# Three edits at the end of attention, and two splits of q in other steps

## The chip, the cores and the metric

The kernel runs on one core of one Trainium2 chip. Five engines work side by side, each through its own list of instructions in order: PE (TensorE) multiplies matrices and turns tiles, DVE (VectorE) and ACT (ScalarE) do elementwise work, POOL (GpSimd) does a little of it and issues some transfers, SP (SyncE) issues most transfers. They meet at semaphores. The metric is the device time of one execution, in microseconds (us): a median over runs. Beside it stands one profiled execution, whose trace gives every instruction's start and length; all rows below are from that trace, in us from the start of its span.

## What is computed

One block of a streaming encoder over 1024 tokens of width 1024, all in float32; branch a is the gated convolution `ya`, branch b causal attention `yb` with 8 heads of 64:

```python
def mixer(h, w_in, b_f, conv_w, w_branch, w_out):
    ...
    proj = jnp.einsum("bsd,dn->bsn", h, w_in)
    q, k, v, f_logit, g_b, g_c, hc, gate_conv, gate_attn = jnp.split(proj, _SPLITS, axis=-1)
    ya = g_b * causal_depthwise_conv(g_c * hc, conv_w)
    ...
    logf = jax.nn.log_sigmoid(f_logit.astype(jnp.float32) + b_f.astype(jnp.float32))
    yb = forgetting_attention(q.reshape(shp), k.reshape(shp), v.reshape(shp), logf)
    yb = yb.reshape(bsz, s_len, ATTN_WIDTH)
    ya_d = jnp.einsum("bsc,cd->bsd", ya, w_branch[0])
    yb_d = jnp.einsum("bsc,cd->bsd", yb, w_branch[1])
    merged = jax.nn.sigmoid(gate_conv) * ya_d + jax.nn.sigmoid(gate_attn) * yb_d
    return jnp.einsum("bsd,de->bse", merged, w_out)
...
        h = rmsnorm(x, norm_mix_pre[l])
        m = mixer(h, w_in[l], b_f[l], conv_w[l], w_branch[l], w_out[l])
        x = x + rmsnorm(m, norm_mix_post[l])
        h = rmsnorm(x, norm_ffn_pre[l])
        f = swiglu(h, w_gate_up[l], w_down[l])
        x = x + rmsnorm(f, norm_ffn_post[l])
```

## The kernel before

Every float32 product is made of three products of split operands: a tensor is cut into a high part (copied on ACT) and a low part (the rest, subtracted on DVE), and PE adds high by high, high by low and low by high into one bank (`mm3`, line 125). The stages are: norm and v; the input projections (which store q, k, `ya` and the gates to DRAM); attention, with branch a's products filled in between; branch b; the output projection with its norms; the gated feed-forward.

**The attention loop** (line 1236) has 24 units of work, `NU`, and runs over steps t from 2 to 25. A unit is a pair of heads j and one or two blocks of 128 rows (`steps`, line 880): heads 0 to 2 have six units each, from row block 7 down to the pair (1, 0), and the last pair has the units 18 to 23. The loop is a pipeline. In step t PE makes the scores of unit t (`sp`), turns the rows of unit t - 1 (`tps`, the weights after the exponential, in 128x128 tiles, up to four to a bank) and multiplies the turned rows of unit t - 2 by v (`pv_pair`, into `po`). DVE adds the bias and takes row maxima (`pt,nm<-sp,cb`), ACT takes the exponentials, and both copy turned rows out of their banks (`ptT<-tps`; `turn_bank` issues the turns and returns the copy as a function; `da` to `dd` are the four of one step, first head then second). In this stage `strict` holds all five engines to the order in which the program is written.

**What fills the steps.** Branch a is cut into groups (d, n): 128 output columns d by 512 tokens n, each in four quarters of three products (`branch_a`, line 1099, tile `pba`). The table `units` gives how many quarters a step takes. The quarters go into one bank, `mb`, one group after the other; the last quarter of a group returns a function, the multiply of the bank by a gate into `um`, and this frees the bank. A step's quarters are issued ahead of `dc` and `dd`. What is left of the step, in this order, is the copies `dc` and `dd`, the exponentials, then three lists:

```python
        for f in lows + muls + at.pop(t, []):
            f()
```

`lows` are the subtractions of the splits whose copies were made earlier in the step (table `cuts`: splits of q, k, `ya` and weights), `muls` are the multiplies, and `at` holds loads and a few others (tables at lines 1200 to 1234). Loads of `raw` tiles share three buffers.

**The inverse rows.** When a pair of heads has all its row sums, DVE takes their reciprocals (`ri`), PE turns them (`tr<-ident,ri`), DVE copies them (`rT`), SP stores them (`ri_dram`) and loads them back spread over the partitions (`rb`), and DVE multiplies `yb` by them (`divide`). For the last pair the reciprocal is in step 24 and the turn in step 25, `NU + 1`.

**Banks.** PSUM has eight here. The pool `pst` (line 671) has two, `ma` (holds `po`) and `mb`; `pss` (line 994) has six, four for scores (`S`) and two for turned tiles (`T`). After the loop both pools close, and `psm2` (line 1291) hands out all eight in turn. Its first three tiles are the three groups of branch a that are left, (7, 0), (6, 1) and (7, 1), between the splits of `yb` and the last divides; then come the groups of branch b (`pbb`).

Of the kernel before, what the change touches and what calls it, by code (L numbers as in the profile page):

```python
# [10 lines left out]
F32 = mybir.dt.float32  # L11
# [6 lines left out]
P = 128  # L18
# [4 lines left out]
NC = 512  # L23
# [22 lines left out]
def block_kernel(  # L46
# [16 lines left out]
    n1, n2 = slice(0, NC), slice(NC, S)  # L63
# [29 lines left out]
    def pool(name, bufs=1, side="left", space=None):  # L93
        kw = dict(name=name, bufs=bufs)
        if space is not DRAM:
            kw["reuse_waits"] = "tile"
        if space is not None:
            kw["space"] = space
        else:
            kw["side"] = side  # L100
        stack = ExitStack()
        ctx.callback(stack.close)
        return stack.enter_context(tc.tile_pool(**kw)), stack.close
# [10 lines left out]
    def mul(o, a, b):  # L114
        nc.vector.tensor_tensor(o, a, b, op=ALU.mult)
# [4 lines left out]
    def split(hi, lo, src):  # L120

        copy(hi, src)
        sub(lo, src, f32(hi))

    def mm3(ps, a, b, start, stop, **kw):

        ah, al = a
        bh, bl = b
        nc.tensor.matmul(ps, ah, bh, start=start, stop=False, **kw)
        nc.tensor.matmul(ps, ah, bl, start=False, stop=False, **kw)  # L130
        nc.tensor.matmul(ps, al, bh, start=False, stop=stop, **kw)

    cpool, _ = pool("const")
    stat, _ = pool("stat", 4, side="right")
    dpool, _ = pool("dram", space=DRAM)
# [355 lines left out]
    wpool, _ = pool("w")  # L491
# [134 lines left out]
    def strassen(w, hb, psp, tmp, p1=None):  # L626

        b1 = None
        if p1 is None:
            b1 = bank(psp, "b1")  # L630
            prod(b1, w["A11"], hb[B11], True)
            p1 = t_(tmp, "c21")
            copy(p1, b1)
        b2, b3 = bank(psp, "b2"), bank(psp, "b3")
        prod(b2, w["S2"], hb[T2], True)
        c12 = t_(tmp, "c12")
        add(c12, p1, b2)
        prod(b3, w["S1"], hb[T1], True)
        c22 = t_(tmp, "c22")
        add(c22, p1, b3)  # L640
        if b1 is not None:
            prod(b1, w["A12"], hb[B21], False)
        prod(b2, w["S3"], hb[T3], False)
        add(c22, c22, b2)
        prod(b3, w["S4"], hb[B22], False)
        add(c12, c12, b3)
        prod(b2, w["A22"], hb[T4], False)
        c21 = p1
        add(c21, p1, b2)
        return b1, c12, c21, c22  # L650
# [21 lines left out]
    psm, psm_close = pool("psm", 6, space=PSUM)  # L672
# [121 lines left out]
    def groups(t):  # L794

        rows_ = steps[t][1]
        if len(rows_) == 1:
            return [[(rows_[0], 0)], [(rows_[0], 1)]]
        return [[(i, 0), (i, 1)] for i in rows_]
# [4 lines left out]
    def mask_of(t, i):  # L804

        j = steps[t][0]
        for e in range(2):
            c = row_of(j, i, e)[:, i * P : (i + 1) * P]
            nc.gpsimd.tensor_tensor(c, c, mask, op=ALU.add)
# [72 lines left out]
    NU = len(steps)  # L882
    sps, nms, ps_, ptTs = {}, {}, {}, {}

    def step_qk(t):
        j, rows_ = steps[t]
        if j not in rsums:
            rsums[j] = t0_.tile([P, 2 * ST], F32, tag="rsum", name="rsum", bufs=2)
        for i in rows_:
            sps[t, i] = qk(j, i)  # L890
# [56 lines left out]
    for ij, (kind, j, _, _) in enumerate(jobs):  # L947
# [4 lines left out]
        if ij < 2:  # L952
# [29 lines left out]
            _, c12, c21, c22 = strassen(w, h1b, psm, pp, p1)  # L982
# [7 lines left out]
        else:  # L990
# [3 lines left out]
            pss, pss_close = pool("pss", space=PSUM)  # L994
# [104 lines left out]
    def branch_a(d, n, psp, tag):  # L1099

        ns = (n1, n2)[n]
        ps = psp.tile([P, NC], F32, tag=tag, name="pba")
        wh, wl = was[d]
        for k in range(4):
            mm3(
                ps, (wh[:, k, :], wl[:, k, :]), (ya2[n][0][:, k, :], ya2[n][1][:, k, :]),
                k == 0, k == 3,
            )
            yield None if k < 3 else lambda: mul(um[:, d, ns], sgs[d, n], ps)
# [16 lines left out]
    def inverse_rows(j, psp, tag, bufs=1):  # L1126

        tr = psp.tile([P, 4, P], F32, tag=tag, name="tr", bufs=bufs)[: 2 * ST, 0, :]
        nc.tensor.transpose(tr, invs[j], ident)

        def drain():
            rT = t1.tile([2 * ST, P], F32, tag="rT", name="rT", bufs=2)
            nc.vector.tensor_copy(rT, tr)
            for e in range(2):
                nc.sync.dma_start(
                    ri_dram[j][e].rearrange("(i p) -> i p", p=P), rT[e * ST : (e + 1) * ST, :]
                )
            rb = rbs[j] = tp_.tile([P, S], F32, tag="rb", name="rb", bufs=1)
            for e in range(2):
                nc.sync.dma_start(  # L1140
                    rb[e * HD : (e + 1) * HD, :], ri_dram[j][e].partition_broadcast(HD)
                )

        return drain
# [3 lines left out]
    def pv_pair(t):  # L1148
        j, rows_ = steps[t]
        k0 = 0  # L1150
        for i in rows_:
            if i % 4 == 3:
                po[0] = pst.tile([P, 4, P], F32, tag="ma", name="po")
            for k in range(i + 1):
                for e in range(2):
                    nc.tensor.matmul(
                        po[0][e * HD : (e + 1) * HD, i % 4, :],
                        vs_[j][:, k, e * HD : (e + 1) * HD],
                        ptTs[t, e][:, k0 + k, :],
                        start=(k == 0),  # L1160
                        stop=(k == i),
                    )
            k0 += i + 1
            if i % 4 == 0:
                copy(
                    yb[:, j, i * P : (i + 4) * P].rearrange("p (a b) -> p a b", a=4),
                    po[0],
                )
# [27 lines left out]
    def do(f, *args):  # L1196
        return lambda: f(*args)
# [1 line left out]

    cuts, at = defaultdict(list), defaultdict(list)  # L1200
    for j, parts in (
        (1, ((2, "k", n1), (3, "k", n2), (4, "q", n2), (5, "q", n1))),
        (2, ((9, "k", n1), (10, "k", n2), (11, "q", n2), (13, "q", n1))),
        (3, ((14, "k", n1), (15, "q", n1), (16, "k", n2), (17, "q", n2))),
    ):
        cuts[parts[0][0]].append(do(qk_tiles, j))
        for t, what, c in parts:
            cuts[t].append(do(split_q if what == "q" else split_k, j, c))
# [8 lines left out]
    at[2].append(do(q_load, 1))  # L1217
    for t, j in ((7, 2), (13, 3)):
        at[t] += [do(load_kv, j), do(q_load, j)]
    for t, n, m in ((2, 0, 0), (3, 0, 2), (3, 1, 0), (6, 1, 2)):  # L1220
        at[t].append(do(load_ya, n, m))
    for d, t in enumerate((2, 6, 8, 11, 13, 17, 20, 23)):
        at[t].append(do(load_wa, d))
# [12 lines left out]
    for t in range(2, NU + 2):  # L1236
        turned = None
        now = groups(t) if t < NU else ([], [])
        back = t - 1 if t <= NU else None
        wide = back and sum(i + 1 for i in steps[back][1]) > 6  # L1240
        if t < NU:
            step_qk(t)
        if 6 < t <= NU:
            pv_pair(t - 2)
        if t in rows:
            turned = inverse_rows(rows[t], pst, "mb")
        if t == NU + 1:
            inverse_rows(3, pss, "T", 2)()
        if back:
            da = turn_bank(back, 0, 0, "ACT")  # L1250
            db = turn_bank(back, 0, 1, "DVE")
            da()
        if t <= 6:
            pv_pair(t - 2)
        for i, e in now[0]:
            row_max(t, i, e)
        if t < NU and len(steps[t][1]) > 1:
            mask_of(t, steps[t][1][1])
        if turned:
            turned()  # L1260
        if back and db:
            db()
        if t == NU:
            inverse(3)
        for i, e in now[0]:
            expo(t, i, e)
        lows = [f for f in (g() for g in cuts.pop(t, ())) if f]
        muls = [m for m in (next(fill, None) for _ in range(units.get(t, 0))) if m]
        if back:
            dc = turn_bank(back, 1, 0, "ACT" if wide else "DVE")  # L1270
            dd = turn_bank(back, 1, 1, "DVE" if wide else "ACT")
        for i, e in now[1]:
            row_max(t, i, e)
        if back:
            dc()
            if dd:
                dd()
        for i, e in now[1]:
            expo(t, i, e)
        if t > NU:  # L1280
            pv_pair(t - 2)
        if t + 1 < NU:
            mask_of(t + 1, steps[t + 1][1][0])
        for f in lows + muls + at.pop(t, []):
            f()
# [5 lines left out]
    psm, psm_close = pool("psm2", 8, space=PSUM)  # L1291
    t1_close()

    def yb_split(n, ks):
        ns = (n1, n2)[n]
        for k in ks:
            split(yb2[n][0][:, k, :], yb2[n][1][:, k, :], yb[:, k, ns])

    for m in branch_a(KT - 1, 0, psm, "mm"):
        pass  # L1300
    for n in range(2):
# [187 lines left out]
    for f in range(NF):  # L1489
        if f < NPRE:  # L1490
# [4 lines left out]
            _, g2, u1_, u2 = strassen(rest.get(), hb, psm, fp, p1)  # L1495
# [270 lines left out]
```

## Time and profile before

| | us |
|---|---|
| median of 3 runs | 1341.31 (1341.25 to 1341.66) |
| the profiled execution's own time | 1342.25 |
| its span | 1340.5 |
| PE busy | 1322.3 (99%) |
| DVE busy | 935.7 (70%) |
| ACT busy | 540.2 (40%) |
| POOL busy | 127.8 (10%) |

A row of a timeline gives the start, the length, the engine, the line, the operation, out<-in, the shape and a count; a bracket at its end gives how long the engine had been idle just before and what ended that. All rows have line 75, which is the helper through which every instruction is recorded, so names tell the place. Products of PE overlap: one starts about 0.23 us after another but is shown as 0.39 long. A row of SP is the issue of a transfer, not the transfer.

### The profile page before, as it was taken

How to read it: one execution, taken by the hardware profiler on the slowest of the kernel's cores; microseconds unless marked ns; L12 is line 12 of the kernel's file. 1: busy time of each engine (PE TensorE's matmuls, PEld its weight loads, DVE VectorE, ACT ScalarE, POOL GpSimd, SP SyncE). 2: the span in 40 equal slices, each digit the busy share in tenths (PEclk: the TensorE clock that was granted, in tenths of full speed). 3: DMA queues.
4: the chain of work that ended last, by engine and by line, in shares of the span. 5: the costliest groups of instructions: out<-in, count | busy, mean ns of one | idle time of the engine just before them, and what ended most of it. 6: DMA issues, size and time to landing. Idle time of an engine off the chain costs nothing. (4 is left out here: it accounts for less than half of the span.)

```text
span 1340.5 us, 17724 instructions
## 1 busy us (share of the span) xinstructions
PE 1322.3 (99%) x6737; PEld 1096.9 (82%) x6737; DVE 935.7 (70%) x1464; ACT 540.2 (40%) x879; POOL 127.8 (10%) x252
## 2 busy tenths in 40 slices
PE   8999999999999999999999999999999999999997
PEld 7988888888887888788887788888888888888886
DVE  6983767755446767675669898677677766677585
ACT  8641322143346756514446322223222323444452
POOL 0011000011112212000002121110011001000000
PEclk9999999999999999999999999999999999999999
DMA  6342422343325445362235554332333336966541
GB/s 206 99 130 87 138 60 82 116 121 99 108 89 173 158 142 190 110 213 79 95 121 186 180 195 143 104 116 75 105 111 110 102 103 248 366 231 197 158 166 63
DMA packets 153558, 186.88 MB, mean 139 GB/s; under 512 B 9448, under 2 KB 106800, under 8 KB 153472
## 3 DMA queue, kind: packets, MB, share of 16 engines
q1 hardware_dynamic: 138736, 137.20, 32.9%
q0 software_dynamic: 14736, 48.54, 9.4%
q8 instruction: 53, 0.87, 0.3%
q14 instruction: 33, 0.27, 0.1%
HBM read 136.62 MB, written 49.09 MB: 139 GB/s over the span
## 5 line engine op out<-in xcount | busy, mean ns | idle before, releaser
L75 DVE TENSOR_TENSOR c<-c,b 128x512 f32<-128x512 f32 x195 | 133.2, 683 | 87.3 <-PE b L75 68.4
L75 DVE TENSOR_TENSOR lo<-raw,hi 128x1024 fp32r<-128x1024 f32 (+1 forms) x93 | 112.1, 1206 | 80.9 <-PE b L75 69.0
L75 ACT ACTIVATE hi<-raw 128x1024 fp32r<-128x1024 f32 (+1 forms) x100 | 101.9, 1019 | 124.6 <-PE b L75 77.2
L75 ACT ACTIVATE hi<-sx 128x1024 fp32r<-128x1024 f32 x41 | 43.6, 1063 | 237.3 <-PE b L75 209.2
L75 PE MATMUL b<-hth,hi 128*128 128x512 f32 x352 | 137.1, 389 | 0.3 <-DVE c L75 0.3
L75 PE MATMUL b<-hth,lo 128*128 128x512 f32 x352 | 137.1, 389 | 0.2 <-DVE lo L75 0.2
L75 PE MATMUL b<-htl,hi 128*128 128x512 f32 x352 | 137.0, 389 | 0.0
L75 PEld LDWEIGHTS b<-hth,hi 128*128 128x128 f32 x352 | 66.1, 188 | 14.5 <-DVE c L75 0.7
L75 PEld LDWEIGHTS b<-hth,lo 128*128 128x128 f32 x352 | 66.1, 188 | 14.2 <-DVE lo L75 0.6
L75 PEld LDWEIGHTS b<-htl,hi 128*128 128x128 f32 x352 | 66.1, 188 | 13.7
L75 DVE TENSOR_TENSOR lo<-sx,hi 128x1024 fp32r<-128x1024 f32 x41 | 50.2, 1224 | 30.8 <-PE b L75 29.4
L75 PE MATMUL b<-hah,hi 128*128 128x512 f32 x176 | 68.7, 393 | 1.5 <-ACT c L75 1.5
L75 PE MATMUL b<-hal,hi 128*128 128x512 f32 x176 | 68.5, 389 | 0.0
L75 PE MATMUL b<-hah,lo 128*128 128x512 f32 x176 | 68.4, 389 | 0.0
L75 DVE TENSOR_TENSOR sx<-raw 128x512 f32<-128x512 f32 x78 | 53.7, 689 | 19.1 <-DMA raw<-in_w_in_dram 8.8
L75 PE MATMUL pd<-hi,lo 128*128 128x512 f32 x160 | 62.3, 389 | 0.0
L75 PE MATMUL pd<-hi 128*128 128x512 f32 x160 | 61.9, 390 | 0.0
L75 PE MATMUL pd<-ghi 128*128 128x512 f32 x148 | 57.6, 390 | 0.0
L75 PE MATMUL pd<-glo,ghi 128*128 128x512 f32 x148 | 57.6, 389 | 0.0
L75 PE MATMUL pd<-ghi,glo 128*128 128x512 f32 x148 | 57.6, 389 | 0.0
L75 PE MATMUL b<-hT34h,hi 128*128 128x512 f32 x136 | 53.0, 390 | 0.4 <-DVE c L75 0.4
L75 PE MATMUL b<-hT34h,lo 128*128 128x512 f32 x136 | 52.9, 389 | 0.0
(380 smaller groups left out, 3366.6 us busy)
## 6 DMA issues: line engine op xcount, KB each, us to landing
raw<-in_w_gate_up_dram SPq DMA_DIRECT2D x51, 512.0 KB, 3.8
raw<-in_w_in_dram SPq DMA_DIRECT2D x35, 512.0 KB, 3.8
a_dramS<-um POOLq DMA_DIRECT2D x44, 256.0 KB, 2.7
a_dramA<-um POOLq DMA_DIRECT2D x33, 256.0 KB, 2.8
sg<-sg_dram SPq DMA_DIRECT2D x32, 256.0 KB, 4.5
xt<-in_x_dram SPq DMA_DIRECT2D x15, 512.0 KB, 4.6
graw<-a_dramS SPq DMA_DIRECT2D x14, 512.0 KB, 3.9
sg_dram<-c POOLq DMA_DIRECT2D x24, 256.0 KB, 2.3
```

What stands on the lines that cost most here:

```text
L75: ins = getattr(self.engine, name)(*args, **kw)
```

## The change

Four edits:

1. In step 24 the multiply that frees branch a's bank is issued at once behind the quarters, ahead of the copies `dc` and `dd` and of the step's subtractions.
2. In step 25 the turn of the last pair's inverse rows, with its copy, stores and loads, is issued behind that step's quarters and not ahead of them.
3. Behind the loop two tiles are taken from `psm2` and not used, so that the groups left get its third, fourth and fifth banks.
4. The split of q's first half for pair 1 moves from step 5 to step 7, with one load of two `ya` tiles moved from step 6 to 7; that of q's second half for pair 2 moves from step 11 to 10.

```diff
@@ -1199,8 +1199,8 @@
 
     cuts, at = defaultdict(list), defaultdict(list)
     for j, parts in (
-        (1, ((2, "k", n1), (3, "k", n2), (4, "q", n2), (5, "q", n1))),
-        (2, ((9, "k", n1), (10, "k", n2), (11, "q", n2), (13, "q", n1))),
+        (1, ((2, "k", n1), (3, "k", n2), (4, "q", n2), (7, "q", n1))),
+        (2, ((9, "k", n1), (10, "k", n2), (10, "q", n2), (13, "q", n1))),
         (3, ((14, "k", n1), (15, "q", n1), (16, "k", n2), (17, "q", n2))),
     ):
         cuts[parts[0][0]].append(do(qk_tiles, j))
@@ -1217,7 +1217,7 @@
     at[2].append(do(q_load, 1))
     for t, j in ((7, 2), (13, 3)):
         at[t] += [do(load_kv, j), do(q_load, j)]
-    for t, n, m in ((2, 0, 0), (3, 0, 2), (3, 1, 0), (6, 1, 2)):
+    for t, n, m in ((2, 0, 0), (3, 0, 2), (3, 1, 0), (7, 1, 2)):
         at[t].append(do(load_ya, n, m))
     for d, t in enumerate((2, 6, 8, 11, 13, 17, 20, 23)):
         at[t].append(do(load_wa, d))
@@ -1244,8 +1244,6 @@
             pv_pair(t - 2)
         if t in rows:
             turned = inverse_rows(rows[t], pst, "mb")
-        if t == NU + 1:
-            inverse_rows(3, pss, "T", 2)()
         if back:
             da = turn_bank(back, 0, 0, "ACT")
             db = turn_bank(back, 0, 1, "DVE")
@@ -1266,6 +1264,11 @@
             expo(t, i, e)
         lows = [f for f in (g() for g in cuts.pop(t, ())) if f]
         muls = [m for m in (next(fill, None) for _ in range(units.get(t, 0))) if m]
+        if t == NU:
+            while muls:
+                muls.pop()()
+        if t > NU:
+            inverse_rows(3, pss, "T", 2)()
         if back:
             dc = turn_bank(back, 1, 0, "ACT" if wide else "DVE")
             dd = turn_bank(back, 1, 1, "DVE" if wide else "ACT")
@@ -1296,6 +1299,8 @@
         for k in ks:
             split(yb2[n][0][:, k, :], yb2[n][1][:, k, :], yb[:, k, ns])
 
+    for _ in range(2):
+        psm.tile([P, NC], F32, tag="mm", name="pba")
     for m in branch_a(KT - 1, 0, psm, "mm"):
         pass
     for n in range(2):
```

DVE, from the last copies of step 24 to the multiplies behind step 25 (`wb` splits write `lo`; `s4l` is the low part of branch a's weights for d = 7):

```order
 L75 COPY ptT<-tps 128x128
 L75 RECIPROCAL ri<-rsum 128x16
+L75 TENSOR_TENSOR um<-sg,pba 128x512
 L75 COPY ptT<-tps 128x512
 L75 TENSOR_TENSOR lo<-raw,hi 128x1024
-L75 TENSOR_TENSOR um<-sg,pba 128x512
 L75 COPY rT<-tr 16x128
 L75 TENSOR_TENSOR s4l<-s_5255,s4h 128x512
```

The multiply goes past the copy and the subtraction; the copy `rT` keeps its place. On PE, the turn `tr` stood between the five turns of step 24 and the twelve products of step 25, and now follows these. The last of those products and what comes behind:

```order
 L75 MATMUL pba<-yl_3539,s4h 128x512
 L75 MATMUL pba<-yh_3538,s4l 128x512
+L75 MATMUL tr<-ident,ri 16x128
 L75 MATMUL po<-ptT,v 64x128 x10
 L75 MATMUL pba<-yh_3538,s4h 128x512
```

So on PE `tr` has moved to just ahead of the last `po`. DVE in step 10, from k's subtraction to step 11's row maxima:

```order
 L75 TENSOR_TENSOR kl<-kl,hi 128x1024
+L75 SCALAR_TENSOR_TENSOR lo<-raw,hi 128x512
 L75 TENSOR_TENSOR um<-sg,pba 128x512
 L75 ISA pt,nm<-sp,cb 128x256
 L75 ISA nm 128x1
```

The subtraction of q's split, which stood behind step 11's last copy of turned rows, now stands ahead of step 10's multiply. On SP the order at the end of attention was load of `sg` for (7, 0), load of `w_out`, load of `sg` for (7, 1), two stores `ri_dram`, a load of `sg` for branch b, two loads of `rb`; it is now both loads of `sg`, `w_out`, the two stores, the two loads of `rb`, then `sg` for branch b. In step 7 SP has the two loads of `ya` behind q's load for pair 2; before, they were issued in step 6, ahead of the loads of weights, gates, bias rows, k and v for the steps to come.

## The prediction

> **What bounds the kernel now.** I read the page first, for the engine that is never idle, then PE's waits, then the timelines around each wait that the edits touch.
>
> ```profile
> span 1340.5 us, 17724 instructions
> PE 1322.3 (99%) x6737; PEld 1096.9 (82%) x6737; DVE 935.7 (70%) x1464; ACT 540.2 (40%) x879; POOL 127.8 (10%) x252
> ...
> PE pba L75 <- DVE um L75: 1.8, 1, 1.8
> ...
> PE pba L75 <- ACT yb L75: 0.7, 1, 0.7
> ...
> PE sp L75 <- DVE lo L75: 0.6, 1, 0.6
> ```
>
> PE is busy 1322.3 of 1340.5 us, so the kernel shortens only where PE's work shrinks (the change takes none away) or where one of PE's few waits goes. In its list of waits the rows are waiter, releaser, total, times, longest; the list is short, and these three are the larger ones in and just behind the attention loop. PE's timeline gives the place of the first two and of a smaller one ahead of them:
>
> ```profile
> 545.82 0.39 PE L75 MATMUL pba<-yh,s4l 128*128 128x512 f32 x1
> 546.05 0.71 PE L75 MATMUL tps<-ident,pt 128*128 128x128 f32 x5
> 547.13 0.28 PE L75 MATMUL tr<-ident,ri 128*16 128x128 f32 x1 [0.37 <-ACT ptT L75]
> 549.16 0.50 PE L75 MATMUL pba<-yh,s4h 128*128 128x512 f32 x1 [1.76 <-DVE um L75]
> ...
> 551.79 0.39 PE L75 MATMUL pba<-yh,s4l 128*128 128x512 f32 x1
> 552.11 1.31 PE L75 MATMUL po<-ptT,v 128*64 128x128 f32 x20
> 554.12 0.50 PE L75 MATMUL pba<-yh,s4h 128*128 128x512 f32 x1 [0.70 <-ACT yb L75]
> ```
>
> and DVE's, ACT's and SP's say why:
>
> ```profile
> 546.69 0.69 DVE L75 COPY ptT<-tps 128x512 f32<-128x512 f32 x1 [2.72 <-PE tps L75]
> 547.30 1.22 DVE L75 TENSOR_TENSOR lo<-raw,hi 128x1024 fp32r<-128x1024 f32 x1
> 548.43 0.68 DVE L75 TENSOR_TENSOR um<-sg,pba 128x512 f32<-128x512 f32 x1
> ...
> 549.23 0.67 DVE L75 TENSOR_TENSOR s4l<-s,s4h 128x512 fp32r<-128x512 f32 x1
> ...
> 552.21 0.69 DVE L75 TENSOR_TENSOR um<-sg,pba 128x512 f32<-128x512 f32 x1 [1.18 <-PE pba L75]
> ...
> 560.50 0.69 DVE L75 TENSOR_TENSOR yb<-yb,rb 128x512 f32<-128x512 f32 x1
> ...
> 553.47 0.60 ACT L75 ACTIVATE yb<-po 128x512 f32<-128x512 f32 x1 [4.93 <-PE po L75]
> ...
> 549.55 0.63 SPq L75 DMA_DIRECT2D ri_dram<-rT  x2
> ```
>
> Branch a's bank is full at 546.21 (545.82 + 0.39), but the multiply that empties it stands on DVE behind a copy of turned rows and a weight split and ends at 549.11; PE's next product group needs that bank and waits to 549.16. Before the next group but one PE waits for ACT to copy `po` (553.47 to 554.07): the first bank of the new pool is the one `po` was in.
>
> **The change part by part.**
>
> *The multiply moved ahead.* DVE had idled 2.72 us before 546.69, so the multiply can start when the bank is full. At 552.21 such a multiply began 0.03 us after its last product (551.79 + 0.39 = 552.18); so here 546.24, end 546.93, and PE resumes 0.05 us later, as from 549.11 to 549.16: at 546.98 instead of 549.16, **2.18 us** saved. PE's five transposes still run under it (546.05 to 546.76); 0.22 us of wait stays. Behind the multiply on DVE, the copy of turned rows is late by some 0.2 us, to about 547.5; it is read by `po` after 550, so this is free.
>
> *The turn of the inverse rows after the products.* It ran inside a wait; now it stands in line between products and `po`:
>
> ```profile
> 485.05 0.28 PE L75 MATMUL tr<-ident,ri 128*16 128x128 f32 x1
> 485.17 0.60 PE L75 MATMUL tps<-ident,pt 128*128 128x128 f32 x4
> ```
>
> It takes 0.12 us of PE in line, at most its 0.28; I take **+0.12**. Its wait for ACT's `ptT` is gone at 549.9. It adds a wait on DVE: `rT` now comes at about 550.2, and `s4l`, the wide `lo` and the next multiply queue behind it. `s4l` then ends near 551.1. PE's order from 546.98 is 2.95 us of products (549.16 to 552.11), 0.12, and 1.31 of `po`: the next group starts at 551.36, and its third product is the first to read `s4l`, 0.45 us later at 551.8. Covered by 0.7 us; were `rT` a microsecond later this would cost 0.3.
>
> *The inverse rows' loads.* `rT` is about 1.2 us later, so both `ri_dram` stores go at 550.5, not 549.55. On SP a load of `sg`, which waits for a multiply, stood between those stores and the loads of `rb`; it now stands behind them. An earlier turn shows the pace without it, and the last row the landing times of all `rb` loads:
>
> ```profile
> 452.75 0.62 SPq L75 DMA_DIRECT2D ri_dram<-rT  x2
> 454.21 1.15 SPq L75 DMA_DIRECT2D rb<-ri_dram  x2
> ...
> DMA to landing us min/median/max: 3.5/4.4/4.4
> ```
>
> 1.46 us from store to load, 0.55 to the second load, 4.4 to landing: 556.9. The divide that reads it was at 560.50 and is wanted 2.76 us sooner, at 557.7. Free, by 0.8 us.
>
> *Other banks.* Two tiles taken and not used put the three last products on the third to fifth banks. By the code the first two are `po`'s and branch a's (that pool was opened first), the next four held scores. The scores' last reader:
>
> ```profile
> 539.03 0.81 DVE L75 CUSTOM_DVE_ANT_0 pt<-sp,cb 128x640 f32<-128x640 f32 x1
> ```
>
> It is done by 540, so the wait of **0.70** goes whole. All later tiles shift by two of eight, with the same distance between uses: nothing.
>
> End of attention: -2.18 + 0.12 - 0.70 = **-2.76 us** (bounds -2.88, the turn free, and -2.2, the turn at 0.28 and `s4l` late by 0.4).
>
> [...] The wait sits in a stretch without ordinary products:
>
> ```profile
> 546.10:549.10 3.00, 0.94 (x7) 0.51 (x5) 2.41 (x4) 1.74 (x3) 0.00 (x0) 1.00 0.00 0
> ```
>
> The columns are length, busy PE, PEld, DVE, ACT, POOL, then granted clock (1.00), DMA share, GB/s. [...] The sum stays by the row; a halved clock, which would make it larger by 2.95 us, is rival E.
>
> *The two splits of q.* Rows first:
>
> ```profile
> 435.08 0.33 PE L75 MATMUL tps<-ident,pt 128*128 128x128 f32 x1 [0.17 <-ACT pt L75]
> ...
> 444.25 1.97 PE L75 MATMUL po<-ptT,v 128*64 128x128 f32 x32
> ...
> 466.07 0.47 PE L75 MATMUL pba<-yh,s4h 128*128 128x512 f32 x1
> ...
> 471.09 0.50 PE L75 MATMUL sp<-hi,lo 64*128 64x512 f32 x2 [0.58 <-DVE lo L75]
> ...
> 464.99 0.68 DVE L75 TENSOR_TENSOR um<-sg,pba 128x512 f32<-128x512 f32 x1
> ...
> 433.54 0.62 ACT L75 ACTIVATE hi<-raw 128x512 fp32r<-128x512 f32 x1
> ...
> 443.15 0.57 ACT L75 ACTIVATE ptT<-tps 128x512 f32<-128x512 f32 x1
> ...
> 455.14 1.14 ACT L75 ACTIVATE yh<-raw 128x512 fp32r<-128x512 f32 x2
> ...
> 463.36 0.28 ACT L75 ACTIVATE ptT<-tps 128x128 f32<-128x128 f32 x1 [0.81 <-PE tps L75]
> ...
> 443.36 4.80 SPq L75 DMA_DIRECT2D raw<-qk_dram  x1
> ```
>
> From step 5 goes ACT's 0.62 us at 433.54, ahead of the exponentials that PE waits for at 435.08: **-0.17**. In step 7 it delays ACT's `ptT` from 443.15 by some 0.5 us, to end near 444.25, just when `po` starts: 0 to +0.2; ACT's chain starts earlier too, so I take 0. In step 10 ACT has 0.81 us idle for the other split. On DVE its subtraction, as long as the multiply itself (0.68, some 0.6 in line), now stands ahead of the multiply of 464.99, which so ends at 466.27; PE wants the bank at 466.07: **+0.25** (bounds 0, if DVE had run ahead, and 0.33). Behind the multiply queue step 11's row maxima, which have until the scores of step 12. In step 12 the split is long done: **-0.58**. The two loads of `ya` pass behind q's load on SP, whose issue took 4.80 us; they go at about 448.2 and land in 4.4 us, as `rb` did, at 453; wanted at 455.14. Sum **-0.50** (bounds -0.75 and 0).
>
> **Total** -3.26. On the profiled execution's own 1342.25 us (span 1340.5) that is 1339.0; that execution stands 0.94 us over the median of the runs, 1341.31, so the runs should show 1338.05; I say **1338.0**, own range 1337.7 to 1339.1. It carries on to the end if nothing later is fixed in time. PE's next wait is
>
> ```profile
> 723.98 0.50 PE L75 MATMUL b<-hah,hi 128*128 128x512 f32 x1 [1.55 <-ACT c L75]
> ```
>
> and the work behind it hangs on earlier PE work, so it moves along.
>
> **The rivals.**
>
> B, the splits give back what they save: the multiply's delay and ACT's in step 7 each at their worst and the 0.58 replaced by another wait. Against it, each delay falls on an engine with idle time there. Then only the end counts: -2.5, 1338.8.
>
> C, `rb` becomes the wait. PE needs what the divide brings at
>
> ```profile
> 563.77 0.39 PE L75 MATMUL pbb<-yh,hi 128*128 128x512 f32 x1
> ```
>
> and between lie the divide (0.69), a copy on ACT (0.60, as at 553.47) and a subtraction (0.67): from 560.50 that is 562.46, 1.3 us of slack. With the 0.8 above, a landing after 559.0 costs one for one. At twice the 4.4 us, 561.35, 2.35 are lost: -0.9, 1340.4. For it: it is the one chain that the change makes later. Against it, the landing row.
>
> D, slower: `ya`'s loads land late. ACT works in order, so `yh` waits at its head and `ptT` and the exponentials behind it. Twice 4.4 us would put `ya` at 457.0, about 1.9 us late. ACT idled 0.81 us in step 10 and PE's use of its results lies a step ahead, so it decides from about 457.5, then one for one. Landing at 463.5 would cost 6.0 and make the whole slower: +2.7, 1344.0. Against it: in
>
> ```profile
> 446.00:452.00 6.00, 6.00 (x66) 5.01 (x62) 4.10 (x9) 3.96 (x8) 0.88 (x2) 1.00 0.98 363
> ```
>
> the DMA engines are full but move 363 GB/s, and the two loads are 0.52 MB, 1.4 us.
>
> E, the clock: in runs without a profile the old wait may have halved it. If so, twelve products of 2.95 us took twice that, and the gain is 2.95 more, 1335.1. The clock of 1.00 and runs within 0.41 us of each other speak against it.
>
> F, the change doesn't do what it says: the new bank is not free sooner and the 0.70 stays: 1338.75.
>
> **How the numbers follow.** Forecast 0.72, B 0.09, C 0.05, D 0.05, E 0.02, F 0.07. A measurement of this kernel tells about 0.2% from no change, 2.7 us: faster means under 1338.6, slower over 1344.0. Faster: nine tenths of the forecast (0.65), E, and of B and F, which lie at the edge, 0.07: 0.74. Slower: D, 0.05. Within: the rest, 0.21. The likeliest's own range, half a microsecond wider below for small waits that go unseen and above for B and F together, gives 1337.2 to 1339.7; C, D and E are left out.
>
> **What would show it.** In the new profile: the first of step 25's products starts under 0.3 us after the transposes; `tr` right behind them without a wait; no wait of a `pba` product for ACT's `yb`; none of `sp` for DVE's `lo`; a new wait of a `pba` product for DVE's `um` of about 0.25 us near 466. A wait for `s4l`, for `yh` in the first `pbb` products or in ACT on `ya` would prove the sum wrong, and so would PE's wait near 721 growing by what was saved.

## The result, and the profile after

The changed kernel took 1339.51 us (median of 16 runs, 1337.97 to 1342.28) and the kernel before, run beside it, 1342.16 us (16 runs, 1340.38 to 1346.17): a ratio of 0.998, 95% interval 0.9972 to 0.9988. It is faster by 2.65 us, where 3.26 were forecast. The median lies inside the forecast's wider range (1337.2 to 1339.7) and above the range of its sum (1337.7 to 1339.1). The profiled execution took 1338.93 us with a span of 1337.2; before, 1342.25 and 1340.5.

The page after, busy times, and then the list of PE's waits (waiter, releaser, total, times, longest):

```profile
span 1337.2 us, 17724 instructions
PE 1321.7 (99%) x6737; PEld 1096.8 (82%) x6737; DVE 935.8 (70%) x1464; ACT 539.7 (40%) x879; POOL 127.3 (10%) x252
```

```profile
PE b L75 <- ACT c L75: 1.6, 1, 1.6
...
PE pba L75 <- ACT yb L75: 0.7, 1, 0.7
...
PE pba L75 <- DVE um L75: 0.2, 1, 0.2
PE po L75 <- DVE ptT L75: 0.2, 1, 0.2
```

PE's work is the same 6737 instructions. The wait for `um` fell from 1.8 to 0.2, the wait of `sp` for `lo` (0.6) is off the list, and the wait of `pba` for ACT's `yb`, 0.7, which was to go, is still there. PE's timeline at the end of attention:

```profile
545.00 0.71 PE L75 MATMUL tps<-ident,pt 128*128 128x128 f32 x5
545.94 0.50 PE L75 MATMUL pba<-yh,s4h 128*128 128x512 f32 x1 [0.23 <-DVE um L75]
...
548.80 0.27 PE L75 MATMUL tr<-ident,ri 128*16 128x128 f32 x1
549.00 1.31 PE L75 MATMUL po<-ptT,v 128*64 128x128 f32 x20
551.01 0.50 PE L75 MATMUL pba<-yh,s4h 128*128 128x512 f32 x1 [0.70 <-ACT yb L75]
```

and DVE's there:

```profile
545.20 0.69 DVE L75 TENSOR_TENSOR um<-sg,pba 128x512 f32<-128x512 f32 x1 [2.29 <-PE pba L75]
545.80 0.68 DVE L75 COPY ptT<-tps 128x512 f32<-128x512 f32 x1
546.40 1.21 DVE L75 TENSOR_TENSOR lo<-raw,hi 128x1024 fp32r<-128x1024 f32 x1
549.11 0.28 DVE L75 COPY rT<-tr 16x128 f32<-16x128 f32 x1 [1.49 <-PE tr L75]
549.32 0.67 DVE L75 TENSOR_TENSOR s4l<-s,s4h 128x512 fp32r<-128x512 f32 x1
...
551.05 0.67 DVE L75 TENSOR_TENSOR um<-sg,pba 128x512 f32<-128x512 f32 x1
...
557.39 0.69 DVE L75 TENSOR_TENSOR yb<-yb,rb 128x512 f32<-128x512 f32 x1
```

The multiply now starts as the bank fills, products resume 0.23 us behind the transposes, and `tr` follows them without a wait. `s4l` ends at 549.99, well before the group at 551.01 wants it. That group starts before DVE has read branch a's old bank (`um` at 551.05), so it doesn't wait for all the banks of the closed pools, and what it waits for is the copy of `po` alone.

Where the time went is read by stretches of PE's timeline between landmarks that both kernels have:

| from, to | before | after | difference |
|---|---|---|---|
| start, first scores of step 4 (424.66; 424.37) | 424.66 | 424.37 | -0.29 |
| to first `pba` product of step 12 (474.20; 473.17) | 49.54 | 48.80 | -0.74 |
| to first `pba` product of step 24 (543.23; 542.18) | 69.03 | 69.01 | -0.02 |
| to the first `pbb` product (562.41; 559.31) | 19.18 | 17.13 | -2.05 |
| to the start of the last product (1333.39; 1330.06) | 770.98 | 770.75 | -0.23 |

Only the second and fourth rows hold edits: 2.79 us. No edit touches the rest, 0.54 us of this pair of executions. That the two spans differ by 3.3, nearly the sum forecast, is therefore chance. (The execution before has a fall of the granted clock to 0.50 near its start, from 12.39 to 15.80, and the one after has none before its last product; this first row shows only 0.29 us of difference.)

### The profile page after: what moved, and what is told of

Same layout as the page of the kernel before. It is cut to its first block, busy times and chain, and to the rows that moved or that the text cites. A ratio compares the mean times of both kernels' runs of the same rounds, so it can differ in the third digit from the quotient of the medians.

```text
span 1337.2 us, 17724 instructions
## 1 busy us (share of the span) xinstructions
PE 1321.7 (99%) x6737; PEld 1096.8 (82%) x6737; DVE 935.8 (70%) x1464; ACT 539.7 (40%) x879; POOL 127.3 (10%) x252
## 3 DMA queue, kind: packets, MB, share of 16 engines
q0 software_dynamic: 14736, 48.54, 9.5%
```

## The experiments

Twelve runs; each edit is shown against the kernel it starts from. "The end" below is the stretch from the first `pba` product of step 24 to the first `pbb` product (19.18 us before, 17.13 after).

**Edits 1 and 2 alone, on the kernel before.**

```diff
-        if t == NU + 1:
-            inverse_rows(3, pss, "T", 2)()
...
+        if t == NU:
+            while muls:
+                muls.pop()()
+        if t > NU:
+            inverse_rows(3, pss, "T", 2)()
         if back:
             dc = turn_bank(back, 1, 0, "ACT" if wide else "DVE")
```

> The kernel before with only the two edits at the end of the loop: the multiply of step 24 ahead of the copies, and the turn of the inverse rows behind the products of step 25. The splits of q and the unused tiles are as before. Between PE's first product of step 24 (543.23 in the kernel before) and its first product of branch b (562.41) lie 19.18 us before and 17.13 in the changed kernel. Theory 1 (the unused tiles do nothing, the first group behind the loop stays in the bank of po): this kernel shows the same 17.1, with the 0.70 us wait for ACT's copy of po still in it, and the stretch of the splits (from the scores of step 4 at 424.66 to the first product of step 12 at 474.20, 49.54 us) stays at 49.5 +- 0.15. Theory 2 (the unused tiles do something that the 0.70 us wait hides): the stretch at the end is longer than 17.5. Total by theory 1: 2.05 us less than the kernel before.

Measured: 1340.15 us against 1343.40, ratio 0.9978 (0.9969 to 0.9987). The end is 17.13, just as in the whole change, with 0.23 us of wait for `um` and 0.69 for `yb`; steps 4 to 12 are as before (49.56). The two edits make all that the end gained, and edit 3 adds nothing to it.

**Edit 1 alone** (the first three of those added lines).

> The kernel before with only the multiply of step 24 moved ahead; the turn of the inverse rows stays ahead of the products of step 25. Theory 1: the turn still waits for ACT's copy of turned rows, which ends 0.3 us behind PE's last transpose, so PE waits about 0.35 for the turn and the products start 0.05 to 0.15 behind it with the bank long free: the stretch at the end is 17.1 to 17.4, that is, the turn's new place brings at most 0.3 of the 2.05. Rival (the turn's place is needed for the gain, since its wait for a bank of turned tiles holds PE up to the copy on DVE): 17.7 or more.

Measured: 1340.29, ratio 0.9977 (0.9966 to 0.9987); the end is 17.17. The multiply carries the gain; edit 2 on top brings 0.04.

**Edit 2 alone** (the rest of those lines).

> Before with the turn of the inverse rows behind step 25's products alone. Theory 1: this edit by itself saves nothing, since PE still waits for the multiply: 19.2 to 19.3 us from the first pba of step 24 to the first pbb with a clock of 1.00, or about 20.9 if a window of 3.41 us holds under half of PE work there, which is likelier than before, as the wait has no turn in it any more. Rival: it brings 0.2 or more by itself.

Measured: one execution, 1343.71 us; the end is 19.30, 0.12 longer than before, with the wait for `um` now 2.40 long since the turn no longer stands in it. Alone it costs its 0.12 us in line. With the multiply ahead it gains 0.04 (17.17 to 17.13): there the turn would have stood ahead of the products and waited 0.37 us for ACT's `ptT`.

**Edit 4 alone.**

```diff
-        (1, ((2, "k", n1), (3, "k", n2), (4, "q", n2), (5, "q", n1))),
-        (2, ((9, "k", n1), (10, "k", n2), (11, "q", n2), (13, "q", n1))),
+        (1, ((2, "k", n1), (3, "k", n2), (4, "q", n2), (7, "q", n1))),
+        (2, ((9, "k", n1), (10, "k", n2), (10, "q", n2), (13, "q", n1))),
...
-    for t, n, m in ((2, 0, 0), (3, 0, 2), (3, 1, 0), (6, 1, 2)):
+    for t, n, m in ((2, 0, 0), (3, 0, 2), (3, 1, 0), (7, 1, 2)):
```

> The kernel before with only the two splits of q (and the load of ya) moved. Theory 1: the stretch from the scores of step 4 to the first product of step 12 falls from 49.54 us to 48.8, as in the changed kernel (-0.74), and the end of attention stays at 19.2. Theory 3 (the prediction's sum, and the rest of the -0.74 is scatter between two executions): 49.04 (-0.50). Total: 0.5 to 0.75 us less than before, within what timing can tell.

Measured: steps 4 to 12 take 48.83 us, where the whole change took 48.80. But the median, 1342.82 against 1343.40, ratio 0.9997 (0.9987 to 1.0006), shows no gain, and the profiled execution is 0.8 us longer than the profiled one of the kernel before. Its end is 20.79 us, where no edit is. PE's timeline there, in this run:

```profile
546.64 0.28 PE L75 MATMUL tr<-ident,ri 128*16 128x128 f32 x1 [0.37 <-ACT ptT L75]
548.68 0.50 PE L75 MATMUL pba<-yh,s4h 128*128 128x512 f32 x1 [1.76 <-DVE um L75]
549.02 0.57 PE L75 MATMUL pba<-yl,s4h 128*128 128x512 f32 x1
549.38 0.63 PE L75 MATMUL pba<-yh,s4l 128*128 128x512 f32 x1
549.81 0.63 PE L75 MATMUL pba<-yh,s4h 128*128 128x512 f32 x1
550.23 0.63 PE L75 MATMUL pba<-yl,s4h 128*128 128x512 f32 x1
```

The waits are those of the kernel before to the hundredth, but the products behind them start 0.43 us apart and not 0.23. The windows of the same run (length, busy PE, PEld, DVE, ACT, POOL, granted clock, DMA share, GB/s) say why:

```profile
545.66:549.07 3.41, 1.28 (x9) 0.81 (x8) 2.87 (x5) 1.74 (x3) 0.00 (x0) 1.00 0.07 5
549.07:552.49 3.42, 3.42 (x10) 2.64 (x9) 1.48 (x2) 0.00 (x0) 0.00 (x0) 0.50 0.69 232
552.49:555.90 3.41, 2.71 (x27) 1.97 (x26) 0.69 (x1) 1.30 (x2) 0.00 (x0) 1.00 0.21 60
```

Behind the old wait the granted clock fell to a half for 3.41 us and cost 20.79 - 19.18 = 1.61 us. Rival E of the prediction is thus real in some executions of a kernel with the old wait, though not in the profiled one of the kernel before.

**The two splits apart**: the change to pair 1 with its load alone, and the change to pair 2 alone (the lines above).

> Before with the split for pair 1 alone (step 5 to 7, with the loads of ya). Read from the first scores of step 4 to the first pba product of step 11: 41.41 us before. Theory 1 (step 5's wait of 0.17 goes and ACT starts its chain earlier, nothing is given back in step 7): 41.2 or less, and the stretch from there to step 12's first pba product stays at 8.13 with the wait of 0.58 for DVE's lo in it. Theory 2 (this part brings nothing, ACT's ptT in step 7 is late by what step 5 gained): 41.4, and a wait of PE in step 7 for ptT; the 0.74 us of the two splits then all come from pair 2.

> Before with the split for pair 2 alone (step 11 to 10). Theory 1 (the multiply in step 10 is late by the subtraction put ahead of it): the first stretch (scores of step 4 to pba of step 11) grows from 41.41 to about 41.65 with a wait of pba for DVE's um of about 0.25, and the second (pba of step 11 to pba of step 12) falls from 8.13 to about 7.35, 0.2 more than the 0.58 of the wait; together 49.0 against 49.54. Theory 2 (the second stretch gives back only its wait): 7.55, together 49.2 with the 0.25 in it.

Measured, one execution each. Pair 1: the first stretch is 41.22, the second 8.12 with the 0.58 in it; 0.19 us saved. Pair 2: 41.70 and 7.29, together 48.99; 0.29 given back at step 11 and 0.84 gained at step 12. The first theory held in both by these numbers; that pair 1 gives nothing back in step 7 did not hold, as its balance further down shows. Pair 2 gains more than the 0.58 of its bracket: in the timeline before, the product that waited started 0.98 us behind the one ahead of it (470.11 to 471.09),

```profile
470.11 0.40 PE L75 MATMUL sp<-kl,hi 64*128 64x512 f32 x2
471.09 0.50 PE L75 MATMUL sp<-hi,lo 64*128 64x512 f32 x2 [0.58 <-DVE lo L75]
471.43 0.40 PE L75 MATMUL sp<-hi 64*128 64x512 f32 x2
```

and in the changed kernel 0.23 us (469.94 to 470.17):

```profile
469.60 0.50 PE L75 MATMUL sp<-hi 64*128 64x512 f32 x2
469.94 0.39 PE L75 MATMUL sp<-kl,hi 64*128 64x512 f32 x2
470.17 0.40 PE L75 MATMUL sp<-hi,lo 64*128 64x512 f32 x2
470.39 0.40 PE L75 MATMUL sp<-hi 64*128 64x512 f32 x2
```

The bracket counts idle time from the shown end of a product (0.40 long), while in the changed kernel the next starts after 0.23; and the product behind the wait is followed after 0.34 and not 0.22 (471.09 to 471.43; 470.17 to 470.39). By this 0.58 cost 0.75 + 0.12 = 0.87 us, against 0.84 measured. The pair 1 run also shows the fall of the clock behind the old wait (0.50 from 548.14 to 551.56; its end is 20.81); the pair 2 run does not (19.18; its fall to 0.50 stands behind a later wait, at 723.63).

**A bank that is really another**: the changed kernel, with the unused tiles gone and (7, 0) in a bank of turned tiles, its multiply issued before the pools close.

```diff
-    def branch_a(d, n, psp, tag):
+    def branch_a(d, n, psp, tag, **kw):
...
-        ps = psp.tile([P, NC], F32, tag=tag, name="pba")
+        ps = psp.tile([P, NC], F32, tag=tag, name="pba", **kw)
...
+    for m in branch_a(KT - 1, 0, pss, "T", bufs=2):
+        pass
+    for n in range(2):
+        nc.scalar.activation(sgs[KT - 1, n], sgs[KT - 1, n], AF.Sigmoid)
+    m()
     pss_close()
     pst_close()
...
-    for _ in range(2):
-        psm.tile([P, NC], F32, tag="mm", name="pba")
-    for m in branch_a(KT - 1, 0, psm, "mm"):
-        pass
-    for n in range(2):
-        nc.scalar.activation(sgs[KT - 1, n], sgs[KT - 1, n], AF.Sigmoid)
-    m()
```

> The changed kernel, but the first group behind the loop takes a bank of the turned tiles (pool pss, tag T) and is finished before the pools close, in place of the two unused tiles. Theory 1 (its bank is po's, and the wait is for that bank): PE's wait of 0.70 us for ACT's copy of po goes, and the stretch at the end falls from 17.13 to 16.4 us; total 0.7 us less than the changed kernel. Theory 4 (PE waits there for something else that ends with ACT's copy): the 0.70 stays and the stretch is 17.1.

Measured: 1339.01 against 1343.40, ratio 0.9967 (0.9955 to 0.9979); the end is 16.35, 0.78 us under that of the change. PE's timeline of this run, where the group behind the last `po` starts:

```profile
547.76 1.31 PE L75 MATMUL po<-ptT,v 128*64 128x128 f32 x20
549.01 0.50 PE L75 MATMUL pba<-yh,s4h 128*128 128x512 f32 x1
549.35 0.39 PE L75 MATMUL pba<-yl,s4h 128*128 128x512 f32 x1
```

There is no bracket. The cause of the old wait was as predicted, the bank of `po`; the edit that was to avoid that bank left the wait in place. This execution lost its gain later: the wait for ACT's `c` near 719 was 2.00 us long and the clock behind it was 0.50, from 719.60 to 723.01.

**Multiplies ahead of subtractions in every step**, on the kernel of the run before.

```diff
-        for f in lows + muls + at.pop(t, []):
+        for f in muls + lows + at.pop(t, []):
```

> The changed kernel with (7, 0) in a bank of turned tiles (as in the run before), and in every step of the loop the multiply that frees branch a's bank ahead of the step's subtractions. Theory 1: the wait of about 0.25 us for um that the split of pair 2 made ahead of step 11 goes, the stretch from the scores of step 4 to the pba of step 12 is 48.55 against 48.80, and the median lies 0.2 us under that of the run before it, about 4.5 to 4.7 us under the kernel before. Rival: the subtractions come late by 0.7 us in every step and waits of sp for lo, or of pba for yl or s4l, take its place: 48.8 or more.

Measured: 1338.57 (5 runs) against 1343.62, ratio 0.9962 (0.9948 to 0.9975), with the shortest profiled span, 1335.8. Steps 4 to 12 take 48.54 and the end 16.37, as expected: the delay that edit 4 had put on the multiply of step 10 is gone and no wait has come in its place. It has the lowest median here, though the 0.3 us of that stretch is too little for medians of 5 and 6 runs to tell it from the run before.

**A longer wait**: the kernel before with step 24's subtraction done twice ahead of the multiply.

```diff
-        for f in lows + muls + at.pop(t, []):
+        for f in lows + (lows if t == NU else []) + muls + at.pop(t, []):
```

> Before, with step 24's subtraction of 1.22 us done twice on DVE, ahead of the multiply for which PE waits: the gap between products grows from 2.95 to about 4.2 us. Read from the first pba of step 24 to the first pbb: 19.18 us before, 20.79 in the run with the two splits alone, where the clock fell behind this gap. Theory 1 (a gap that is long enough halves the granted clock, and at 2.95 us that depends on the run): the clock is low behind the gap in this profile, products there start 0.43 us apart for some 3 us, and the stretch is 22.0 us or more (1.22 of the delay and 1.6 or more of the clock); in the median it costs 2.5 us or more. Rival (the fall has nothing to do with the gap's length): 20.4, products 0.23 us apart, and 1.2 us in the median.

Measured: 1345.23 against 1343.62, ratio 1.0007 (0.9998 to 1.0016): 1.6 us by the medians, 0.9 by the ratio (0.3 less to 2.1 more), which is short of the first theory's 2.5 and holds the rival's 1.2. The profile is as the first theory had it: the end is 22.02, with a clock of 0.50 from 552.08 to 555.49. Its windows, cut at the edges of its two falls:

```profile
545.26:548.67 3.41, 1.97 (x12) 1.29 (x10) 1.79 (x2) 1.68 (x3) 0.00 (x0) 1.00 0.00 0
548.67:552.08 3.41, 1.47 (x6) 1.24 (x7) 3.38 (x6) 0.06 (x1) 0.00 (x0) 1.00 0.29 59
552.08:555.49 3.41, 3.41 (x13) 2.32 (x13) 0.97 (x2) 0.00 (x0) 0.00 (x0) 0.50 0.47 179
...
12.78:16.19 3.41, 3.41 (x17) 3.41 (x17) 2.73 (x9) 2.87 (x6) 0.00 (x0) 0.50 0.87 354
```

The clock fell 1.47 us after the products had resumed (552.08 against 550.61), behind a stretch in which PE was busy for 1.47 of 3.41 us. The same execution has a fall near the start, the last row. That the median lost less may be because the kernel it is compared with has such falls too; only the profile, one execution, speaks for the first theory.

**The same, with PE kept busy in the wait** by turning the last inverse rows 18 times into the same place.

```diff
-        nc.tensor.transpose(tr, invs[j], ident)
+        for _ in range(18 if j == 3 else 1):
+            nc.tensor.transpose(tr, invs[j], ident)
```

> The run with the doubled subtraction, and in PE's wait the turn of the last inverse rows is done 18 times instead of once (the same rows into the same place, some 2 us of PE work that ends before the multiply does). The gap between products stays at 4.2 us. Theory 1 (the clock falls behind a window of 3.41 us in which PE is busy for less than about half, turns counted as busy): no window there holds under 2.3 us of PE work, the clock is 1.00 behind the gap, and the stretch from the first pba of step 24 to the first pbb is 20.4. Rival (turns don't count, a gap between products of 4.2 us is what halves the clock): low clock behind the gap, 22.0 as in the run with the doubled subtraction alone.

Measured: the end is 20.44. PE's timeline and windows of this run:

```profile
545.93 2.13 PE L75 MATMUL tr<-ident,ri 128*16 128x128 f32 x18 [0.37 <-ACT ptT L75]
549.23 0.50 PE L75 MATMUL pba<-yh,s4h 128*128 128x512 f32 x1 [1.16 <-DVE um L75]
549.56 0.40 PE L75 MATMUL pba<-yl,s4h 128*128 128x512 f32 x1
```

```profile
544.18:547.60 3.42, 3.05 (x25) 2.36 (x24) 2.08 (x3) 1.74 (x3) 0.00 (x0) 1.00 0.00 0
547.60:551.01 3.41, 2.25 (x13) 1.64 (x11) 3.41 (x5) 0.00 (x0) 0.00 (x0) 1.00 0.36 80
551.01:554.42 3.41, 2.71 (x27) 2.00 (x26) 0.77 (x2) 0.88 (x2) 0.00 (x0) 1.00 0.48 174
```

The gap between products is as long, 4.2 us, and the clock is 1.00 across and behind it: the 1.6 us are the clock's. Of the 3.05 us in the first window, turns make 2.38 (1.67 of `tr`, 0.71 of `tps`); without them it would hold some 0.7, and in the run with the doubled subtraction alone a window with 1.47 us, of products alone (548.67 to 552.08), had a fall behind it. This is one execution: it agrees with the theory that counts turns as work and does not show it.

**The kernel before with the wait filled** (13 turns, no doubled subtraction).

> Before, with the turn of the last inverse rows done 13 times instead of once, all of it inside the wait of 1.76 us. Theory 1 (in about half of the executions of the kernel before the clock fell behind this wait, for 1.6 us): never here; the stretch from the first pba of step 24 to the first pbb is 19.2, and the median lies 0.8 us (half of 1.6) under that of the kernel before, though the multiply comes no sooner. Rival (the falls are rare, or have nothing to do with PE's work in the wait): the medians differ by less than 0.3 us, or the turns cost what they last.

Measured: the end is 19.18 and the clock 1.00 there, but the medians are alike, 1343.36 against 1343.34; by the ratio, 0.9994 (0.9985 to 1.0003), it is 0.8 us less, from 2.0 less to 0.4 more. What the falls behind the old wait cost on average is not settled by these medians.

**The changed kernel once more**, on one chip with these.

> The changed kernel again, beside the kernel before on one chip with the runs of this call. From the stretches of the traces (splits 0.74, end of attention 2.05) the gain without the clock is 2.8 us; Theory 1 adds half of 1.6 us for the falls behind the old wait: 3.6. Rival (only the stretches count): 2.8. The clock in the profile is 1.00 behind step 24's transposes.

Measured: 1340.14 against 1343.34, ratio 0.997 (0.9958 to 0.9982): 3.2 by the medians, 4.0 by the ratio with 2.4 to 5.6, which holds both 2.8 and 3.6. Its stretches repeat the first profile's (48.82 and 17.12, clock 1.00 behind step 24), but the profiled execution took 1344.63, 5.7 us more than the first one of the same kernel. Windows of this run behind two later waits:

```profile
718.43:721.84 3.41, 1.50 (x7) 0.90 (x7) 1.06 (x2) 3.06 (x5) 0.26 (x1) 1.00 0.85 280
721.84:725.25 3.41, 3.41 (x10) 2.64 (x9) 1.89 (x3) 2.81 (x5) 0.83 (x2) 0.50 0.50 164
752.57:755.98 3.41, 1.41 (x6) 1.17 (x7) 3.23 (x6) 1.81 (x3) 0.00 (x0) 1.00 0.15 43
755.98:759.39 3.41, 3.41 (x10) 2.64 (x9) 2.33 (x4) 1.26 (x2) 0.00 (x0) 0.50 0.88 264
```

Two falls stand here where the first profile had none. Ahead of the first PE waited 1.91 us for ACT's `c` (1.64 in the first profile), ahead of the second 2.26 us for DVE's `c`. Such scatter is not this kernel's alone: in 6 of the 14 profiles of this study, of kernels with and without the edits, the clock fell to 0.50 behind the wait for ACT's `c` near 720 us. Why `c` is late in some executions was not tried.

## Why the prediction was right, and where it was wrong

The direction and the bulk were right. The distance of 1.5 us between 1338.0 and 1339.51 has two parts: the kernel before, run 16 times, has a median 0.85 us over that of its first three runs, and the gain was 0.61 less than forecast. That the median still lay in the wider range is partly luck, since two terms were wrong in opposite directions:

- **The multiply moved ahead**: right to a few hundredths, in its place, its size (wait left 0.22 forecast, 0.23 measured) and its cause.
- **The turn behind the products**: right. `s4l`, the inverse rows and the divide were covered: the divide started at 557.39, 3.11 us sooner than before, as the `pbb` products behind it did (3.10). With the multiply the two steps were put at -2.06 and brought -2.05.
- **Other banks**: this is the step that failed. It read "two tiles taken and not used put the three last products on the third to fifth banks". The group (7, 0) still waits for ACT's copy of `po`, for the 0.70 us as before, as rival F had it. The runs show it from both sides: edits 1 and 2 without the unused tiles give the same end of 17.13, and a bank of turned tiles takes the wait away. So the group still had `po`'s bank. That tiles which nothing writes get no bank would explain it; no trace prints a tile's bank, so this reason is argued and not shown. The step took the banks from the order of the program's text alone.
- **The two splits**: right in each mechanism and short in one size: step 12 was put at 0.58, by the bracket, and brought some 0.85. The delay of the multiply came as forecast (0.25; the `pba` product at 465.84 starts 1.00 us behind the transposes ahead of it, and before 0.74; PE's list shows no bracket for it, since the transposes are shown 0.98 long). Pair 1's sum was 0.02 off, by two parts that were each larger: step 5 gained 0.39 (0.87 to 0.48 from its second turns to `po`), and 0.2 was given back in steps 6 and 7, where 0 stood. Sum -0.74 where -0.50 stood. The 0.24 more makes up for a third of what edit 3 did not bring.
- **Nothing later is fixed in time**: right. The wait for `c` moved along (1.55 before; 1.64 after), and the stretch behind the end changed by 0.23 us, within what one kernel scatters there (770.75 in the first profile of the changed kernel, 776.46 in the second).
- **Rival E**, at a chance of 0.02 because the one profile showed a clock of 1.00 and three runs agreed, was ruled out too easily. Of four profiles with the old wait unaltered (before, edit 4, and its two parts) two had the fall. Its price was set at 2.95 us, twelve products at half speed, which no run shows: in these two the clock was 0.50 for 3.41 us and the end 1.61 and 1.63 us longer. The changed kernel shows none there in either profile; its waits there are 0.23 and 0.70 us. If half of the old executions paid 1.6, the change is worth 2.79 + 0.8 = 3.6 on average; the measured 2.65 (1.6 to 3.8 by the ratio) and 4.0 (2.4 to 5.6) can't tell this from 2.79.
- **The mean granted clock**, which stands with every execution, tells more of rival E. It is 0.99693 over 61 executions of the kernel before, and 0.99778 over 55 executions of the six sets with the multiply ahead (both sets of the changed kernel, edits 1 and 2, edit 1, the other bank, multiplies first). The difference, 0.00085 (0.0005 to 0.0012), times 1340 us gives an estimate of 1.1 us (0.6 to 1.7) for what the falls behind the old wait cost on average. The kernel with that wait filled lies with the second group (0.99767, 12 executions) and the splits alone with the first (0.9964, 10). The runs of edit 1 and of edits 1 and 2 agree: by the medians they gained 3.11 and 3.25 us, 1.1 and 1.2 more than their stretches. A mean clock doesn't say where it fell, so the place is argued and not shown, and the exact share of the median stays open.

## What to carry to other kernels

Before giving an edit of banks a price, find out which bank the one instruction that matters really gets; the order of the text did not tell it here. Price a wait on PE by the spacing of the products' starts across it (0.87 us in step 12, where 0.84 was measured) and not by its bracket (0.58). And where a kernel has a PE wait like the 1.76 us here, which had a fall of the clock behind it in two profiles of four, one profile is not enough to say what it costs: look at several, by window, for the granted clock behind it, and at the mean clock of all executions.

## What the runs showed of the hardware

Behind the old wait of 1.76 us a fall of the granted clock cost about as much again in two profiles (edit 4, 1.61 us, and its part for pair 1, 1.63) and nothing in two others, which have no fall there (the kernel before and the part for pair 2). Every fall ahead of the last product was to 0.50 and lasted 3.41 us (17 in the 14 profiles). Not every fall costs time: the second profile of the changed kernel has one near its start, at 11.87, and reaches the scores of step 4 at 424.35, the first has none there and reaches them at 424.37.

PE was not idle in the 3.41 us just ahead of a fall: it was busy for 1.28 us of them in the run of edit 4, 1.47 in that of the longer wait, and 1.41 (the other bank) and 1.50 (the second profile of the changed kernel) ahead of two falls near 720; the most away from the start is this, from the run with 18 turns, ahead of its fall at 725.09:

```profile
721.68:725.09 3.41, 1.60 (x7) 1.02 (x6) 0.96 (x2) 3.23 (x5) 0.43 (x1) 1.00 0.86 264
```

Near the start of the kernel, falls came behind 3.41 us that held 1.73 to 1.99 us. And in the profiled kernel before 3.41 us across the old wait held the same 1.28, and the clock was 1.00 there and behind:

```profile
546.00:549.41 3.41, 1.28 (x8) 0.80 (x7) 2.72 (x5) 1.74 (x3) 0.00 (x0) 1.00 0.00 0
549.41:552.82 3.41, 3.41 (x26) 2.64 (x26) 2.23 (x3) 0.00 (x0) 0.00 (x0) 1.00 0.76 238
```

So the runs show no amount of work at which the clock falls, and why the same wait has a fall behind it in one execution and not in another is open.
